# A rotary step whose halves ScalarE swaps, and one group of queries kept in natural order

## The chip, the cores and the metric

The kernel runs on one core of a Trainium2 chip. A core has TensorE (PE in the profile, with its weight loads shown apart as PEld), VectorE (DVE), ScalarE (ACT), GpSimd (POOL), and SyncE (SP), which here issues all DMAs. The metric is the device time of one execution in microseconds (us).

## The reference

A decoder trunk of two layers over 1024 tokens of width 1024. The first layer is gated linear attention. The second makes keys and values once, projects queries for three groups of eight heads, and lets each group attend through a dilated window; then the groups are mixed by their log sum of exponentials, gated, projected out, and normalized. What the change touches is the rotary step of the keys and queries and the score product:

```python
def rope(x, pos):
    half = e // 2
    ang = pos[:, None] * inv[None, :]          # one angle for each of 64 pairs
    x1, x2 = x[..., :half], x[..., half:]
    return concatenate([x1 * cos - x2 * sin, x2 * cos + x1 * sin])

SWA_GROUPS = ((128, 1), (512, 4), (2048, 16))  # window, dilation of groups 0, 1, 2
# group with dilation d: the sequence is split into d interleaved subsequences
# (t = i*d + r); each is a plain band of 128 keys, swept in blocks of 128 queries
scores = einsum('brnqgpe,brnkge->brngpqk', qb, kcat)
```

The head width is 128, so a head's queries lie with one component on each of the 128 partitions and the tokens along the free dimension. The two halves that the rotary step mixes are partitions 0 to 63 and 64 to 127.

## The kernel before

All large products are made in three matmuls: each fp32 operand is split into a high and a low part (`wh` and `wl` for weights, `x1h` and `x1l` for the residual stream), and high by high, high by low, low by high add up in PSUM (`mm3`, L642). These run in a fast fp32 mode, 512 tokens at a time. The attention products (`lv` scores, `ms` transposes, `po` sums over values) are plain fp32 matmuls; the profile shows each of those as two matmul records with a weight load for each.

Layer B works unit by unit, a unit being one query head in all three groups (`u` from 0 to 7). `q_proj(u)` projects three 128x1024 pages of queries, `Q[0]` to `Q[2]`, each in two halves of 512 tokens. A half is 24 matmuls into one of two PSUM banks (`acc`), and `rope` (L1194) takes it out: DVE multiplies it by the cosines into `t1`, then in two 64-partition instructions multiplies the swapped halves by the sines into `t2`, and DVE or POOL adds the two into the page. The page is stored in the order of its group (`to_group`, L1165): group 0 in token order, group 1 with the four subsequences one after the other (256 tokens each), group 2 in 16 short runs. Keys `K` go through the same `rope`, in 12 halves. `scores(u)` (L1327) multiplies a block of queries, as the stationary operand, with its keys, as the moving one; DVE adds the mask and takes the row extreme, ACT takes the exponential. `attend(u)` scales the probabilities by the mixing weights `cw`, which make a round trip through DRAM, transposes them, and multiplies with the values.

The order of work is made at build time. Every call is recorded with the engines that may run it (`S.vp` is DVE or POOL, `S.va` is DVE or ACT), and `Sched.order` (L254) simulates the engines with a table of costs (`cost`, L543), taking at each step the instruction that can start first, with a priority from program order. So one edit moves many instructions. All instructions are issued at L452, which is why the profile names tiles and not lines. The unit loop is L1515 to L1528: while PE scores unit `u`, its gaps are filled with projections of the next unit.

Of the kernel before, what the change touches and what calls it, by code (L numbers as in the profile page):

```python
# [597 lines left out]
def trunk(tc, xT, wP, wA, wA12, wAv3, w2, wO, wK, wV0, wV12, wB, wOB, par_d,  # L598
          ident_d, lmask_d, cos_d, sin_d, bmask_d, rmask_d, tri_d, lnr_d, out):
    S = Sched(tc, lat=LAT, pad=PAD)  # L600
# [6 lines left out]
    t2 = S.pool("t2")  # L607
    t1 = S.pool("t1", side="right")
# [9 lines left out]
    def page(pool, dt, name):  # L618
        return pool.tile([128, T], dt, name=name, tag="pg", bufs=16)

    def hs(half):
        return slice(half * 512, half * 512 + 512)


    def load_w(src):
        with S.later(-WEIGHTS):
            return load_w_now(src)
# [21 lines left out]
    def proj_cols(w, xs, r, acc):  # L649
        hi, lo = w  # L650
        for kt in range(NK):
            xh, xl = xs[kt]
            mm3(acc, hi[:, kt, :], lo[:, kt, :], xh[:, r], xl[:, r], kt)

    def project(piece, xs, evac, halves=(0, 1)):
        w = load_w(piece)
        for half in halves:
            acc = ps.tile([128, 512], F32, name="acc", bufs=2)
            proj_cols(w, xs, hs(half), acc)
            with S.later(-EVAC):  # L660
                evac(half, acc)
# [391 lines left out]
    def small(name, tag, bufs, dt=F32, shape=(128, 512)):  # L1053
        return hp.tile(list(shape), dt, name=name, tag=tag, bufs=bufs)
# [110 lines left out]
    def to_group(pg, g, half):  # L1165
        if g == 2:
            return pg.rearrange("p (e a n) -> p n a e", e=16, a=8)[:, half * 4:half * 4 + 4]
        n = 512 // DIL[g]
        return pg.rearrange("p (r i) -> p i r", r=DIL[g])[:, half * n:half * n + n, :]

    def tok_view(ap, g):
        if g == 2:
            return ap.rearrange("p (n a e) -> p n a e", n=4, a=8)
        return ap.rearrange("p (i r) -> p i r", r=DIL[g])

    def layer_b(xs, early):
# [14 lines left out]
        sinT = page(p0, F32, "sinT")  # L1191
        S.sync.dma_start(sinT, sin_d)

        def rope(pg, g, half, acc):  # L1194
            r = hs(half)
            t1 = small("t1", "t1", 2)
            S.vector.tensor_mul(t1, acc, cosT[:, r])
            t2 = small("t2", "t2", 2)
            S.vector.tensor_mul(t2[0:64, :], acc[64:128, :], sinT[64:128, r])
            S.vector.tensor_mul(t2[64:128, :], acc[0:64, :], sinT[0:64, r])  # L1200
            S.vp.tensor_add(to_group(pg, g, half), tok_view(t1, g), tok_view(t2, g))

        K = [[page(p0, F32, f"K{c}{g}") for g in range(3)] for c in range(2)]
        V = [[None] * 3 for _ in range(2)]
# [98 lines left out]
        def q_proj(u):  # L1303
            Q = [page(p0, F32, "Q") for _ in range(3)]
            U[u]["Q"] = Q
            for g in range(3):
                project(wB[u, g], xs, lambda half, acc: rope(Q[g], g, half, acc))


        def g_proj(u):  # L1310
# [9 lines left out]

        def pieces(P, g, j0):
            p, o = P[g, j0 + 1]
            n = 1 if g or not j0 else 2
# [2 lines left out]

        def scores(u):  # L1327
            Q, Kc = U[u]["Q"], K[u // 4]
            P = {}
            sts = hp.tile([128, 2, 24], F32, name="sts", bufs=2)  # L1330
            for g in (2, 1, 0):
                step = 8 if g == 2 else 2
                for j0 in range(0, 8, step):
                    sc = ps.tile([128, 512], F32, name="lv", bufs=2)
                    p = small("P", "a", 13)
                    o = 0
                    if g == 2:
                        with S.group():
                            for j in range(8):
                                for s in range(2):  # L1340
                                    x = s * 512 + j * 64
                                    o = place(j)
                                    S.tensor.matmul(sc[s * 64:s * 64 + 64, o:o + 64], Q[g][:, x:x + 64],
                                                     Kc[g][:, x:x + 64], start=True, stop=True)
                    for j in range(j0, j0 + step):
                        qc, kc, nk = BL[g][j]
                        col = column(g, j)
                        if g == 2:
                            o = place(j)
                        P[g, j] = p, o  # L1350
                        px = p[:, o:o + nk]
                        if g < 2:
                            S.tensor.matmul(sc[:, o:o + nk], Q[g][:, qc:qc + 128], Kc[g][:, kc:kc + nk],
                                             start=True, stop=True)
                        mk = rmask if g == 2 else bmask[:, 256 - nk:]

                        S.vector.tensor_tensor_reduce(
                            out=px, in0=sc[:, o:o + nk], in1=mk, scale=-QSCALE, scalar=-LOWEST,
                            op0=OP.add, op1=OP.min, accum_out=sts[:, 0, col:col + 1])
                        S.scalar.activation(px, px, AF.Exp, scale=-1.0, bias=sts[:, 0, col:col + 1],  # L1360
                                             accum_out=sts[:, 1, col:col + 1])
                        o += nk
                    if g < 2:

                        prev, own = pieces(P, g, j0)
                        S.vector.copy_predicated(own, above.to_broadcast(list(own.shape)), prev)
            U[u]["P"] = P

# [232 lines left out]
def _arrays(inputs):  # L1601
    import numpy as np

    f4 = np.float32
    c = np.ascontiguousarray
    w_in = np.asarray(inputs["gla_w_in"])[0]

    def cols(w, first, n=128):

        return w[:, first:first + n].reshape(8, 128, n).transpose(1, 0, 2)  # L1610

    r = np.arange
    w_out = np.asarray(inputs["gla_w_out"])[0]
    w_kv = np.asarray(inputs["w_kv"])
    swi = np.asarray(inputs["swa_w_in"])[0]
    swo = np.asarray(inputs["swa_w_out"])[0]
    w2 = np.asarray(inputs["gla_w_a2"])[0]
    a = {
        "xT": c(np.asarray(inputs["x"])[0].T),
        "wP": c(np.concatenate([cols(w_in, 1024, 256), cols(w_in, 3072, 16)], axis=2)),  # L1620
        "wA": c(np.stack([np.stack([cols(w_in, f) for f in (h * 128, 512 + h * 128, 2048 + h * 256,
                                                             2176 + h * 256)]) for h in range(4)])),
        "wA12": c(cols(w_in, 1280, 512)),
        "wAv3": c(cols(w_in, 1792, 256)),
        "w2": c(np.concatenate([w2] * 6, axis=0)),
        "wO": c(np.stack([cols(w_out, e * 128) for e in range(8)])),
        "wK": c(np.stack([cols(w_kv, e * 128) for e in range(6)])),
        "wV0": c(cols(w_kv, 768, 256)),
        "wV12": c(cols(w_kv, 1024, 512)),
        "wB": c(np.stack([np.stack([cols(swi, f * 1024 + h * 128) for f in range(4)]) for h in range(8)])),  # L1630
        "wOB": c(np.stack([cols(swo, e * 128) for e in range(8)])),
        "par": c(np.concatenate([np.asarray(inputs[n]).reshape(-1, 128).T
                                 for n in ("ln_g", "ln_b", "gla_norm_g", "gla_b_a2")], axis=1)),

        "lnr": c(np.stack([np.broadcast_to(np.asarray(inputs[n])[1], (128, 1024)) for n in ("ln_g", "ln_b")])),
    }

    a["ident"] = np.eye(128, dtype=f4)
    j, i = np.meshgrid(r(128) % 32, r(32), indexing="ij")
    lm = np.zeros((128, NLEV - 2, 32), f4)  # L1640
    for n, L in enumerate(LEVELS[2:]):
        lm[:, n, :] = (j // (2 * L) == i // (2 * L)) & (j % (2 * L) < L) & (i % (2 * L) >= L)
    lm[:, NLEV - 3, :] = j == i
    a["lmask"] = lm
    inv = f4(10000.0) ** (-(r(64, dtype=f4) * f4(2.0)) / f4(128.0))
    ang = r(1024).astype(f4)[None, :] * inv.astype(f4)[:, None]
    cs, sn = np.cos(ang).astype(f4), np.sin(ang).astype(f4)
    a["cos"] = c(np.concatenate([cs, cs]))
    a["sin"] = c(np.concatenate([sn, -sn]))
    q, k = np.meshgrid(r(128), r(256), indexing="ij")  # L1650
    rel = 128 + q - k
    a["bmask"] = np.where((rel >= 0) & (rel <= 128), f4(0), f4(NEG)).astype(f4)
    q, k = np.meshgrid(r(128) % 64, r(64), indexing="ij")
    tq, tk = (128 * (i % 8) + 16 * (i // 8) for i in (q, k))
    i, j = np.arange(128)[:, None], np.arange(128)[None, :]
    a["tri"] = np.stack([j > i, j < i, j >= i], axis=1).astype(f4)
    a["rmask"] = np.where(tk <= tq, f4(0), f4(NEG)).astype(f4)
    return a
# [27 lines left out]
```

## Time and profile before

| what | value |
|---|---|
| time, median of 3 runs | 1154.25 us (1153.87 to 1154.63) |
| span of the profiled execution | 1152.7 us |
| PE busy | 1142.8 us, 99% of the span |
| DVE busy | 820.3 us, 71% |
| ACT busy | 449.1 us, 39% |
| POOL busy | 188.0 us, 16% |

The span runs from the first to the last instruction of one profiled execution; the median lies 1.5 us above it, and that execution has no other time of its own. The busy time of PE counts a matmul until its modelled end, and matmuls overlap, so the pace of PE is read from the distance between starts and not from durations. On the other engines busy time is what the instruction held the engine.

### The profile page before, as it was taken

What the parts mean: (1) busy time and instruction counts of PE and PEld (TensorE: products, weight loads), DVE (VectorE), ACT (ScalarE), POOL (GpSimd) and SP (SyncE); (2) the same over time, 40 slices, a digit from 0 to 9 for tenths busy, and PEclk for the clock granted to TensorE, in tenths of its full rate; (3) what the DMA queues carried; (4) which work ended last, traced back from release to release, by engine and by line L of the source; (5) the groups of instructions that cost most, each with busy time, mean ns of one, the idle gap of its engine ahead of it and who ended that gap; (6) DMA issues with size and microseconds to landing.
All of it is one profiled execution on the core that took longest, in us unless ns stands there. A gap on an engine that the chain in (4) does not pass through costs nothing.

```text
span 1152.7 us, 19731 instructions
## 1 busy us (share of the span) xinstructions
PE 1142.8 (99%) x7780; PEld 975.2 (85%) x7780; DVE 820.3 (71%) x1634; ACT 449.1 (39%) x929; POOL 188.0 (16%) x139
## 2 busy tenths in 40 slices
PE   9999999999999999999999999999999999999997
PEld 9888888889988888888988888888888888888876
DVE  6286862786966699764366868686777878767678
ACT  5355431646463335311214242424222443444342
POOL 1000100112011120211020303030211312212200
PEclk9999999999999999999999999999999999999999
DMA  7211222111144365443611111121141111134544
GB/s 256 71 38 38 74 79 87 38 61 51 57 171 140 137 214 158 166 143 103 208 47 34 51 38 57 38 50 45 38 165 39 38 21 38 39 96 126 193 136 182
DMA packets 93372, 108.39 MB, mean 94 GB/s; under 512 B 43648, under 2 KB 61952, under 8 KB 93280
## 3 DMA queue, kind: packets, MB, share of 16 engines
q1 hardware_dynamic: 93280, 107.13, 29.6%
q8 instruction: 61, 1.00, 0.4%
q14 instruction: 31, 0.25, 0.1%
HBM read 85.94 MB, written 21.17 MB: 93 GB/s over the span
## 4 chain that ended last, share of the span: by engine, by line
PE 93%; DVE 4%; DMA 2%; ACT 1%; issue 1%; POOL 0%; DVEq 0%; ACTq 0%
PE acc L452 63%; PE po L452 9%; PE lv L452 8%; PE vac L452 7%; PE ms L452 4%; PE pro L452 2%; DMA wf<-in_wOB 2%; DVE rt L452 1%; DVE wl L452 1%; DVE x1l L452 0%; ACT wh L452 0%; DVE P L452 0%; DVE lnA L452 0%; ACT woh L452 0%; DVE wol L452 0%
## 5 line engine op out<-in xcount | busy, mean ns | idle before, releaser
L452 PE MATMUL acc<-x1h,wh 128*128 128x512 f32 x608 | 252.3, 415 | 0.0
L452 PE MATMUL acc<-x1h,wl 128*128 128x512 f32 x608 | 237.6, 391 | 0.0
L452 PE MATMUL acc<-x1l,wh 128*128 128x512 f32 x608 | 237.1, 390 | 0.0
L452 ACT ACTIVATE wh<-wf 128x1024 fp32r<-128x1024 f32 (+2 forms) x104 | 108.1, 1040 | 281.0 <-PE acc L452 194.8
L452 POOL TENSOR_TENSOR wl<-wf,wh 128x1024 fp32r<-128x1024 f32 x39 | 93.5, 2397 | 553.1 <-ACT wh L452 414.8
L452 ACT ACTIVATE P<-P,sts 128x128 f32<-128x128 f32 (+2 forms) x192 | 81.5, 426 | 139.6 <-DVE sts L452 139.3
L452 PEld LDWEIGHTS acc<-x1h,wl 128*128 128x128 f32 x608 | 114.1, 188 | 24.5
L452 PEld LDWEIGHTS acc<-x1l,wh 128*128 128x128 f32 x608 | 114.5, 188 | 21.3
L452 PEld LDWEIGHTS acc<-x1h,wh 128*128 128x128 f32 x608 | 114.4, 188 | 21.1
L452 DVE TENSOR_TENSOR wl<-wf,wh 128x1024 fp32r<-128x1024 f32 (+2 forms) x66 | 83.4, 1265 | 58.2 <-ACT wh L452 48.0
L452 PE MATMUL acc<-xh,wh 128*128 128x512 f32 x256 | 101.8, 397 | 0.0
L452 PE MATMUL acc<-xh,wl 128*128 128x512 f32 x256 | 99.8, 390 | 0.0
L452 PE MATMUL acc<-xl,wh 128*128 128x512 f32 x256 | 99.7, 390 | 0.0
L452 DVE TENSOR_TENSOR t<-acc,cosT 128x512 f32<-128x512 f32 x60 | 41.4, 689 | 65.7 <-PE acc L452 65.7
L452 DVE TENSOR_TENSOR t<-acc,sinT 64x512 f32<-64x512 f32 x120 | 82.5, 688 | 1.6
L452 PE MATMUL lv<-K,Q 128*64 128x64 f32 (+2 forms) x512 | 70.2, 286 | 0.0
L452 DVE CUSTOM_DVE_ANT_0 P<-lv,bmask 128x256 f32<-128x256 f32 (+1 forms) x128 | 46.7, 379 | 25.1 <-PE lv L452 23.7
L452 PEld LDWEIGHTS lv<-K,Q 128*128 128x128 f32 (+1 forms) x512 | 53.8, 163 | 10.0 <-issue 1.6
L452 PE MATMUL acc<-ogh,wh 128*128 128x512 f32 x152 | 60.1, 395 | 0.0
L452 PE MATMUL acc<-ogh,wl 128*128 128x512 f32 x152 | 59.2, 389 | 0.0
L452 PE MATMUL acc<-ogl,wh 128*128 128x512 f32 x152 | 59.2, 389 | 0.0
L452 PEld LDWEIGHTS acc<-xh,wl 128*128 128x128 f32 x256 | 48.0, 188 | 10.2
(252 smaller groups left out, 2233.4 us busy)
## 6 DMA issues: line engine op xcount, KB each, us to landing
wf<-in_wB SPq DMA_DIRECT2D x32, 512.0 KB
wf<-in_wA SPq DMA_DIRECT2D x24, 512.0 KB
wf<-in_wO SPq DMA_DIRECT2D x16, 512.0 KB
wf<-in_wOB SPq DMA_DIRECT2D x16, 512.0 KB
wf<-in_wV SPq DMA_DIRECT2D x12, 512.0 KB
res<-in_xT SPq DMA_DIRECT2D x16, 256.0 KB
x1d<-rt SPq DMA_DIRECT2D x16, 256.0 KB
out<-rt SPq DMA_DIRECT2D x16, 256.0 KB
```

The source lines that it names most:

```text
L452: getattr(handle[o.eng], meth)(*[conv(a) for a in args], **{k: conv(v) for k, v in kw.items()})
```

## The change

`rope` makes the swap a job of its own. ACT copies partitions 64 to 127 of the PSUM bank into partitions 0 to 63 of `t2`, and 0 to 63 into 64 to 127; one multiplication over all 128 partitions, on DVE or POOL, then applies the sines, and the addition stays. The sine table changes the sign of its halves to fit. Keys are stored as before. Of the queries, group 1 is now stored in token order, by a plain addition, and `scores` reads each block of its stationary operand with a step of four elements (16 bytes).

```diff
-        def rope(pg, g, half, acc):
+        def rope(pg, g, half, acc, walked=(0, 1, 2)):
             r = hs(half)
             t1 = small("t1", "t1", 2)
             S.vector.tensor_mul(t1, acc, cosT[:, r])
             t2 = small("t2", "t2", 2)
-            S.vector.tensor_mul(t2[0:64, :], acc[64:128, :], sinT[64:128, r])
-            S.vector.tensor_mul(t2[64:128, :], acc[0:64, :], sinT[0:64, r])
-            S.vp.tensor_add(to_group(pg, g, half), tok_view(t1, g), tok_view(t2, g))
+            S.scalar.copy(t2[0:64, :], acc[64:128, :])
+            S.scalar.copy(t2[64:128, :], acc[0:64, :])
+            S.vp.tensor_mul(t2, t2, sinT[:, r])
+            if g in walked:
+                S.vp.tensor_add(to_group(pg, g, half), tok_view(t1, g), tok_view(t2, g))
+            else:
+                S.vp.tensor_add(pg[:, r], t1, t2)
...
-                project(wB[u, g], xs, lambda half, acc: rope(Q[g], g, half, acc))
+                project(wB[u, g], xs, lambda half, acc: rope(Q[g], g, half, acc, (0, 2)))
...
             Q, Kc = U[u]["Q"], K[u // 4]
+            Q = [Q[0], Q[1].rearrange("p (i r) -> p r i", r=4), Q[2]]
...
                         if g < 2:
-                            S.tensor.matmul(sc[:, o:o + nk], Q[g][:, qc:qc + 128], Kc[g][:, kc:kc + nk],
+                            qb = Q[1][:, qc // 256, qc % 256:qc % 256 + 128] if g else blk(Q[0], j)
+                            S.tensor.matmul(sc[:, o:o + nk], qb, Kc[g][:, kc:kc + nk],
                                              start=True, stop=True)
...
-    a["sin"] = c(np.concatenate([sn, -sn]))
+    a["sin"] = c(np.concatenate([-sn, sn]))
```

Layer A keeps its order; in layer B the planner places work anew. Three places of the new order follow.

On DVE, the rotary step of the first half of group 1's queries in unit 1 (`Q_6090` before, `Q_6130` now). Before:

```order
L452 TENSOR_TENSOR t1_6076<-acc_6029,cosT_4371 128x512
L452 TENSOR_TENSOR t2_6081<-acc_6029,sinT_4375 64x512 x2
L452 TENSOR_TENSOR Q_6090<-t1_6076,t2_6081 128x128x4
L452 TENSOR_TENSOR mnB_6095<-nat_5964 128x8
L452 TENSOR_TENSOR mnB_6095<-mnB_6095,sts_5841 128x8
```

Now:

```order
L452 TENSOR_TENSOR t1_6117<-acc_6052,cosT_4371 128x512
L452 TENSOR_TENSOR t2_6119<-t2_6119,sinT_4375 128x512
L452 TENSOR_TENSOR Q_6130<-t1_6117,t2_6119 128x512
L452 TENSOR_TENSOR t1_6156<-acc_6113,cosT_4371 128x512
L452 TENSOR_TENSOR wl_6163<-wf_5976,wh_6154 128x1024
L452 TENSOR_TENSOR t2_6161<-t2_6161,sinT_4375 128x512
```

The two 64-partition products of the PSUM bank have become one product of `t2` with itself as input and output, the addition writes in one run of 512, and a split of weights (`wl`) that POOL made elsewhere stands on DVE.

On ACT, from the last exponential of unit 0 to the mixing weights' scalings (`P<-P,cw`). Before:

```order
L452 ACTIVATE P_6011,sts_5841<-P_6011,sts_5841 128x256 x2
L452 ACTIVATE wh_6033<-wf_5810 128x1024
L452 ACTIVATE ew_6101<-ew_6101 128x24
L452 ACTIVATE wh_6129<-wf_5927 128x1024
L452 ACTIVATE P_5947<-P_5947,cw_6116 128x128
L452 ACTIVATE P_5957<-P_5957,cw_6116 128x256
```

Now, from the copies of the fourth half to those of the fifth:

```order
L452 ACTIVATE t2_6161<-acc_6113 64x512 x2
L452 ACTIVATE P_5949<-P_5949,cw_6104 128x128
L452 ACTIVATE P_5949<-P_5949,cw_6104 128x256
L452 ACTIVATE P_5880<-P_5880,cw_6104 128x128
L452 ACTIVATE P_5880<-P_5880,cw_6104 128x256
L452 ACTIVATE P_5893<-P_5893,cw_6104 128x128
L452 ACTIVATE P_5911<-P_5911,cw_6104 128x128
L452 ACTIVATE P_5928<-P_5928,cw_6104 128x256
L452 ACTIVATE P_5968<-P_5968,cw_6104 128x256
L452 ACTIVATE P_6003<-P_6003,cw_6104 128x256
L452 ACTIVATE t2_6213<-acc_6150 64x512 x2
```

Each half now has a pair of copies in ACT's queue, and the pair of the fifth half (`acc_6150`) stands behind all of ACT's scalings of unit 0.

On PE, scores of group 1 in unit 1 (`K01` are its keys) between the projections. Before:

```order
L452 MATMUL acc_6398<-x1h2_4296,wl_6042 128x512
L452 MATMUL lv_6415<-K01_5008,Q_6090 128x128
L452 MATMUL lv_6396<-K01_5008,Q_6090 128x256
L452 MATMUL acc_6398<-x1h3_4320,wh_6033 128x512
L452 MATMUL acc_6398<-x1l3_4335,wh_6033 128x512
L452 MATMUL acc_6398<-x1h3_4320,wl_6042 128x512
L452 MATMUL lv_6415<-K01_5008,Q_6090 128x256
L452 MATMUL lv_6429<-K01_5008,Q_6090 128x128
```

Now:

```order
L452 MATMUL acc_6417<-x1h1_4254,wl_6066 128x512
L452 MATMUL lv_6370<-K01_5010,Q_6130 128x256
L452 MATMUL lv_6413<-K01_5010,Q_6130 128x256
L452 MATMUL acc_6417<-x1h2_4296,wh_6056 128x512
L452 MATMUL acc_6417<-x1l2_4310,wh_6056 128x512
L452 MATMUL acc_6417<-x1h2_4296,wl_6066 128x512
L452 MATMUL lv_6442<-K01_5010,Q_6130 128x128
```

The same matmuls stand in a slightly other interleaving; each `Q_6130` is the operand read with a step.

## The prediction

> **What bounds the kernel now.** I read the page's first parts, then what PE waits for, then the pace at which PE's matmuls start, then the groups by form.
>
> ```profile
> span 1152.7 us, 19731 instructions
> PE 1142.8 (99%) x7780; PEld 975.2 (85%) x7780; DVE 820.3 (71%) x1634; ACT 449.1 (39%) x929; POOL 188.0 (16%) x139
> ...
> PE 93%; DVE 4%; DMA 2%; ACT 1%; issue 1%; POOL 0%; DVEq 0%; ACTq 0%
> ```
>
> PE is busy for all but 10 us, and 93% of the chain that ended last is PE. Busy time alone proves little, since a matmul's end is modelled. The waits of PE, complete:
>
> ```profile
> PE pro L452 <- DVE Dg L452: 1.2, 1, 1.2
> PE po L452 <- DVE PT L452: 0.8, 1, 0.8
> PE ms L452 <- DVE sum L452: 0.5, 2, 0.2
> PE ms L452 <- ACT sum L452: 0.2, 1, 0.2
> ```
>
> That is 2.7 us in the whole program. The first is the start, the last two the normalizations; only the 0.8 us, in the last unit's `attend`, lies in work that this change moves. A short wait could still hide inside modelled ends, so I checked the pace of starts in layer B:
>
> ```profile
> 710.99 0.39 PE L452 MATMUL acc<-x1l,wh 128*128 128x512 f32 x1
> 711.22 0.39 PE L452 MATMUL acc<-x1h,wl 128*128 128x512 f32 x1
> ...
> 731.15 0.81 PE L452 MATMUL lv<-K,Q 128*128 128x128 f32 x4
> 731.62 0.58 PE L452 MATMUL acc<-x1h,wh 128*128 128x512 f32 x1
> 732.03 0.39 PE L452 MATMUL acc<-x1l,wh 128*128 128x512 f32 x1
> ```
>
> A 512-token matmul starts 0.227 us after the one before, all through. At 731.15 PE leaves the projections for four fp32 score records (two of 128 columns, two of 256) and goes back. From 731.15 to 732.03 are 0.88 us; at 0.112 us for 128 fp32 columns (from rows further down) and twice that for 256 the content is 0.224 + 0.448 + 0.227 = 0.90 us. So going back and forth between the two kinds costs nothing that shows. PE is full, and what DVE does is hidden behind it.
>
> **The change, part by part.** The durations:
>
> ```profile
> L452 DVE TENSOR_TENSOR t<-acc,sinT 64x512 f32<-64x512 f32 x120 | 82.5, 688 | 1.6
> L452 DVE TENSOR_TENSOR t<-acc,cosT 128x512 f32<-128x512 f32 x60 | 41.4, 689 | 65.7 <-PE acc L452 65.7
> L452 DVE TENSOR_TENSOR rt<-rt,R 128x512 f32<-128x512 f32 x24 | 16.0, 683 | 0.3 <-ACT R L452 0.3
> L452 POOL TENSOR_TENSOR Q<-t,t 128x512 f32<-128x512 f32 x8 | 11.3, 1411 | 0.0
> L452 ACT ACTIVATE th<-acc 128x512 f32<-128x512 f32 x16 | 9.4, 588 | 20.6 <-PE acc L452 20.6
> L452 DVE TENSOR_TENSOR wl<-wf,wh 128x1024 fp32r<-128x1024 f32 (+2 forms) x66 | 83.4, 1265 | 58.2 <-ACT wh L452 48.0
> ...
> 686.60 0.69 DVE L452 TENSOR_TENSOR Q<-t,t 128x512 f32<-128x512 f32 x1
> ...
> 698.60 1.09 DVE L452 TENSOR_TENSOR Q<-t,t 128x512 f32<-128x512 f32 x1
> ```
>
> *The products with the sines.* DVE loses 120 instructions of 688 ns, 82.5 us. In their place are 60 products of two SBUF operands over 128 partitions, nearest to the `rt<-rt,R` row: in the new order 51 on DVE at 683 ns (34.8 us) and 9 on POOL at 1.41 us (12.7 us).
>
> *Group 1's additions.* The row at 686.60 is group 0 written in one run, the one at 698.60 is group 1 written with a step of 256 elements: 0.40 us more. Sixteen additions lose it, 6.4 us of DVE and POOL. The planner hands some of the time back: DVE takes 14 weight splits (`wl`, 1.27 us each, 17.7 us) from POOL. DVE ends near 820 - 83 + 35 - 6 + 18, about 785 us, or less busy by 35 us. What it is worth: nothing, because PE waited 0.8 us in all for DVE in this stretch.
>
> *The copies.* 120 of them, 64x512 from PSUM on ACT. No row has this form. `th<-acc`, 512 elements a partition from PSUM, takes 588 ns, and DVE's rows show 64 partitions costing as much as 128 (688 and 689), so I take 588; half of it is a lower bound, and the 688 that DVE needs for the same swapped read an upper one. That is 71 us on ACT, 449 to about 520 of 1152. Cover: a bank is taken again 24 matmuls later, 24 x 0.227 = 5.4 us, while the cosine product and the pair of copies run side by side and free it in 1.2 us, against 0.69 + 2 x 0.69 = 2.1 before. The addition follows after 1.18 + 0.68, no later than before. Worth nothing; if ACT comes late, see the third case.
>
> *The order of PE.* The matmuls are the same. They change between projections and fp32 work oftener (176 stretches of projections against 161 in PE's order); at no cost that shows, or 0.01 us of rounding each, this is at most 0.15 us.
>
> *The strided operand.* 64 score matmuls of group 1 (four subsequences, two blocks, eight units), 128 weight loads, now read their 128 columns with a step of 16 bytes. No load in the trace does. The rows to bound it by:
>
> ```profile
> L452 PEld LDWEIGHTS lv<-K,Q 128*128 128x128 f32 x256 | 45.7, 189 | 7.7
> L452 PEld LDWEIGHTS lv<-K,Q 128*64 128x64 f32 x256 | 8.1, 138 | 2.3 <-issue 1.6 <-DVE zz L452 0.7
> ...
> 720.35 2.40 PE L452 MATMUL po<-PT,V 128*128 128x128 f32 x20
> ...
> 725.31 3.29 PE L452 MATMUL po<-PT,V 128*128 128x128 f32 x28
> ```
>
> A load of 64 columns takes 138 ns and one of 128 takes 189, so a column costs 0.8 ns and a dense load occupies about 102 ns behind the running matmul. The two `po` rows bound it from below: the 20 records at 720.35 are group 1 and write PSUM with just this step of four fp32 elements, the 28 at 725.31 are group 0 and write densely. Spacing: (2.40 - 0.275) / 19 = 0.112 us against (3.29 - 0.275) / 27 = 0.112. On the same engine, the same step at the same pace of under one element per 0.8 ns costs nothing: lower end 0. From above: DVE's stepped addition pays 0.40 / 512 = 0.79 ns more per element; on 128 columns 101 ns, a load of 203. A load hides behind the matmul record in front of it. By the new order, 40 of the 128 loads stand behind a record of 128 fp32 columns (0.112 us), 5 behind a shorter one, all others behind 0.21 us or more: 40 x (203 - 112) + 5 x 101 = 4.1 us. With no cover at all it is 128 x 101 = 12.9 us. I take 0, because the `po` row shares engine, step and pace with the new read, while DVE's row is a write with a 64 times longer step.
>
> **The sum.** 1152.7 span + 0 (DVE) + 0 (ACT) + 0.15 (order) + 0 (loads) = 1152.9; the last unit's wait of 0.8 us may go or double. The shown median lies 1.5 us above the span: 1154.4 us, no change. Own range 1153.4 to 1156.
>
> **The rivals.** *Slower by the strided loads:* the place is the second record of each 128-column score, where the load has only 0.112 us of cover. For: the stepped DVE row, SBUF like this read. Against: the `po` rows. It decides from 2.3 / 45 = 51 ns of exposed time a load, a load of some 165 ns. Price 4.1 us: 1158.5; up to 1167 without cover. The Trainium skill, page "SBUF — State Buffer", section "Specifications (TRN2)", speaks for this case: SBUF has 16-byte lines and full bandwidth needs at least two hits per line, whereas a step of four fp32 gives one. The page "PSUM — Partial Sum Buffer", same section, has a like rule for 8-byte lines, that any non-contiguous pattern slows matmuls significantly; the two `po` spacings of 0.112 us disagree with that one, so I do not let the rule decide.
>
> *Slower by ACT's queue:* the fifth half's copies stand behind nine scalings that wait for the mixing weights from DRAM.
>
> ```profile
> ACT P L452 <- DMA cw<-cwd: 5.0, 2, 4.5
> ...
> 702.13 3.98 ACT L452 ACTIVATE P<-P,cw 128x128 f32<-128x128 f32 x11 [0.48 <-DMA cw<-cwd]
> ```
>
> Eleven scalings take 3.98 us, nine 3.3. If `cw` lands as the half ends, its bank is free 3.3 + 1.2 = 4.5 us later, and PE needs it after another half and eight transposes (16 records), 5.4 + 1.8 = 7.2 us. So 2.7 us are spare. A wait of 4.5 us, the longest here, would stop PE for 1.8 us; two of them in the seven units make 3.6 us: 1158.0. Against: the second wait was 0.5 us.
>
> *Faster:* a less busy DVE removes the 0.8 us wait and rounding in the scores. Beyond that PE has nothing to lose but its 64 stepped matmuls and the 1.9 us at start and normalizations, which the change does not reach. Price 1153.6, within the bound; over 2.3 us it would take a tail that shortens, and there the rows are layer norm's.
>
> *The change doesn't do what it says:* the planner could have kept as many DVE instructions; the order rules it out.
>
> **How the numbers follow.** No change 0.51 (1154.4); strided loads 0.38 (1158.5); ACT's queue 0.05 (1158.0); faster 0.06. The likeliest gives the time. The range reaches to the load case with part of its bounds, 1152.6 to 1161; outside are 6 in 100 below and some 8 above. Faster and slower begin at 0.2%, 2.3 us, about what a measurement of this kernel can tell from no change: faster 0.06, same 0.51, slower 0.38 + 0.05 = 0.43.
>
> **What would show it.** Loads right: `lv<-K,Q` loads of 128 columns stay at 189 ns and PE's spacing inside group 1's scores at 0.112 us; wrong: longer loads, and a second 128-column record that starts 0.2 us after the first. Copies: `t<-acc` on ACT near 588 ns, 120 times. DVE: near 785 us, `Q<-t,t` of group 1 at 0.69. PE's waits stay below 4 us; a new row "PE acc <- ACT t" there would be the third case. The forecast falls if PE's starts thin out anywhere in layer B.

## The result, and the profile after

The changed kernel takes 1164.6 us (median of 4 runs, 1163.9 to 1164.7), the kernel before 1154.1 us in runs beside it (1153.6 to 1154.6). The ratio is 1.0092, with a 95% interval from 1.0078 to 1.0107: slower by about 10.5 us, outside the range of the forecast. The changed kernel's page and TensorE's waits, complete:

```profile
span 1162.9 us, 19850 instructions
PE 1150.4 (99%) x7780; PEld 984.7 (85%) x7780; DVE 781.8 (67%) x1608; ACT 515.8 (44%) x1035; POOL 155.0 (13%) x119
...
PE 92%; DVE 4%; DMA 2%; ACT 1%; issue 1%; SPq 0%; DVEq 0%; ACTq 0%
```

```profile
PE ms L452 <- DVE P L452: 2.6, 3, 0.9
PE pro L452 <- DVE Dg L452: 1.2, 1, 1.2
PE ms L452 <- DVE sum L452: 0.5, 2, 0.2
PE acc L452 <- DVE wol L452: 0.3, 1, 0.3
PE ms L452 <- ACT sum L452: 0.2, 1, 0.2
```

DVE is relieved as planned and ACT takes the copies, but the span is 10.2 us longer and PE is still busy for 99% of it. The waits sum to 4.8 us against 2.7. A row is new: three times the transposes (`ms`) wait for DVE's scaled probabilities (`P`), 2.6 us together, while the 0.8 us for `PT` are gone. So most of the 10 us cannot be a wait that this list shows. The groups by form (busy us, mean ns, idle before and what ended it) show where else to look:

```profile
L452 PEld LDWEIGHTS lv<-K,Q 128*128 128x128 f32 x256 | 57.1, 253 | 7.2 <-DVE sts L452 0.9
L452 PE MATMUL lv<-K,Q 128*128 128x128 f32 x80 | 20.9, 342 | 0.0
L452 ACT ACTIVATE t<-acc 64x512 f32<-64x512 f32 x120 | 71.2, 593 | 92.3 <-DVE t L452 64.8 <-PE acc L452 17.9 <-DVE mnB L452 8.3
L452 DVE TENSOR_TENSOR t<-t,sinT 128x512 f32<-128x512 f32 x51 | 47.7, 935 | 33.2 <-ACT t L452 33.1
```

The score loads take 253 ns on the mean, 189 before. Half of the 256 still read densely, so a stepped one is near 2 x 253 - 189 = 317 ns. The timeline shows what that does to the pace of TensorE, at the first block of a subsequence of group 1 (128 columns, two records):

```profile
663.26 0.63 PE L452 MATMUL lv<-K,Q 128*128 128x128 f32 x2
663.73 0.94 PE L452 MATMUL po<-PT,V 128*128 128x128 f32 x7
```

The two records and their loads fill 663.73 - 663.26 = 0.47 us, or 0.235 us a record; the forecast had 0.112. A busy PE hides this, since a matmul that waits for its weights counts as busy. The lines on ACT hold the second clue, taken up below: the copies were mostly held by DVE's `t`, the cosine product of the same bank.

### The profile page after: what moved, and what is told of

It reads as the page before. It is cut to its first block, busy times and chain, and to the rows that moved or that the text cites. A ratio compares the mean times of both kernels' runs of the same rounds, so it can differ in the third digit from the quotient of the medians.

```text
span 1162.9 us, 19850 instructions
## 1 busy us (share of the span) xinstructions
PE 1150.4 (99%) x7780; PEld 984.7 (85%) x7780; DVE 781.8 (67%) x1608; ACT 515.8 (44%) x1035; POOL 155.0 (13%) x119
## 4 chain that ended last, share of the span: by engine, by line
PE 92%; DVE 4%; DMA 2%; ACT 1%; issue 1%; SPq 0%; DVEq 0%; ACTq 0%
PE acc L452 60%; PE lv L452 10%; PE po L452 9%; PE vac L452 7%; PE ms L452 4%; PE pro L452 2%; DVE rt L452 1%; DMA wf<-in_wOB 1%; DVE wl L452 1%; DMA nat<-std 1%; DVE x1l L452 0%; ACT wh L452 0%; DVE lnA L452 0%; DVE t L452 0%; ACT woh L452 0%
## 5 line engine op out<-in xcount | busy, mean ns | idle before, releaser
L452 DVE TENSOR_TENSOR wl<-wf,wh 128x1024 fp32r<-128x1024 f32 (+2 forms) x80 | 99.7, 1247 | 61.1 <-ACT wh L452 51.1
L452 POOL TENSOR_TENSOR wl<-wf,wh 128x1024 fp32r<-128x1024 f32 x25 | 59.8, 2390 | 556.3 <-PE ms L452 305.0
L452 ACT ACTIVATE t<-acc 64x512 f32<-64x512 f32 x120 | 71.2, 593 | 92.3 <-DVE t L452 64.8
L452 PE MATMUL lv<-K,Q 128*64 128x64 f32 (+2 forms) x512 | 77.7, 299 | 0.0
L452 PEld LDWEIGHTS lv<-K,Q 128*128 128x128 f32 (+1 forms) x512 | 65.2, 195 | 9.2 <-DVE P L452 1.1
L452 DVE TENSOR_TENSOR t<-t,sinT 128x512 f32<-128x512 f32 x51 | 47.7, 935 | 33.2 <-ACT t L452 33.1
```

What stands on the lines that cost most here:

```text
L452: getattr(handle[o.eng], meth)(*[conv(a) for a in args], **{k: conv(v) for k, v in kw.items()})
```

## The experiments

Two theories stood at the start. **Loads:** the 128 stepped weight loads cost TensorE 6 to 7 us, and what is left comes from the new order of the other engines. **Order:** the loads are hidden, and the new order on DVE and ACT thins out TensorE. The diffs below are against the changed kernel; experiments that build on another say so.

### The rotary step alone

```diff
-                project(wB[u, g], xs, lambda half, acc: rope(Q[g], g, half, acc, (0, 2)))
+                project(wB[u, g], xs, lambda half, acc: rope(Q[g], g, half, acc))
...
-            Q = [Q[0], Q[1].rearrange("p (i r) -> p r i", r=4), Q[2]]
...
-                            qb = Q[1][:, qc // 256, qc % 256:qc % 256 + 128] if g else blk(Q[0], j)
+                            qb = Q[g][:, qc:qc + 128]
```

> The rotary step alone: the copies on ScalarE and the one product with the sines as in the change, but group 1's queries go back to group order and the scores read them densely. If the strided loads cost the most (theory: 128 loads at about 310 to 330 ns instead of 190, some 6 to 7 us of TensorE), the time falls to 1156 to 1158 us, since 2 to 4 us of the new order stay, and all 256 loads of 128 columns stand at 189 ns. If it is the new order of VectorE and ScalarE that thins out TensorE (rival), the time stays near 1163.

Measured: 1158.55 us, ratio 1.0037 (1.0023 to 1.0051) to the kernel before, loads at 189 ns. Neither theory had it: just above the first one's 1158, far under the second one's 1163. Without one stepped load the rotary step costs 4.6 us. TensorE's waits in it begin with

```profile
PE ms L452 <- DVE P L452: 4.0, 3, 1.4
```

### The stepped read alone

```diff
             t2 = small("t2", "t2", 2)
-            S.scalar.copy(t2[0:64, :], acc[64:128, :])
-            S.scalar.copy(t2[64:128, :], acc[0:64, :])
-            S.vp.tensor_mul(t2, t2, sinT[:, r])
+            S.vector.tensor_mul(t2[0:64, :], acc[64:128, :], sinT[64:128, r])
+            S.vector.tensor_mul(t2[64:128, :], acc[0:64, :], sinT[0:64, r])
```

(with the sine table of before)

> The other part alone: the rotary step of before (VectorE's 120 half products with the sines), but group 1's queries in natural order, read with a step of 16 bytes. Loads theory: 1160 to 1161 us, the 128 stepped loads at 310 to 330 ns, ScalarE near 449 us. Rival (order): 1154, the same as before, though the loads are longer.

Measured: 1163.69 us, 1.0084 (1.0069 to 1.0099), loads at 254 ns, ACT busy 447 us. The loads cost time whatever the rotary step is; 9.7 us is more than either theory's figure. This kernel's order differs from both others, so the sum of the two parts (4.6 + 9.7) need not be, and isn't, the whole. It has three waits of TensorE that the kernel before lacks, 0.9 us together (for `sts` 0.5, for `sg` and `P` 0.2 each). And its loads are covered less well: 53 of the 128 stepped ones stand behind a record of 128 columns, against 40 in the changed kernel, and 5 behind a shorter one. With 0.235 us for a stepped load an estimate is 53 x 0.123 + 5 x 0.133 us, and up to 0.025 us for each of the other 70: 7.2 to 8.9 us, with the waits 8.1 to 9.8. The 9.7 us lie at its upper end.

### The changed kernel with dense weights

Only the address pattern of the 64 weights differs from the changed kernel; every engine has the same instructions in the same places. Group 1's scores then belong to other tokens' queries.

```diff
-            Q = [Q[0], Q[1].rearrange("p (i r) -> p r i", r=4), Q[2]]
...
-                            qb = Q[1][:, qc // 256, qc % 256:qc % 256 + 128] if g else blk(Q[0], j)
+                            n, r = qc % 256 // 128, qc // 256
+                            qb = Q[1][:, n * 512 + r * 128:n * 512 + r * 128 + 128] if g else blk(Q[0], j)
```

> The changed kernel with every instruction at its place on every engine, but the 64 stepped weights of group 1's scores are taken as 128 neighbouring columns of the same half of the page: group 1's scores then use other tokens' queries than they should, which changes no duration but the load's. Loads theory: 1157 to 1158 us, so 6 to 7 below the change, loads of 128 columns all at 189 ns. Rival (order): 1164, as the change.

Measured: 1157.19 us, 1.0030 (1.0019 to 1.0042). So in an unchanged order the step costs 1164.6 - 1157.2 = 7.4 us, and everything else in the change 3.2 us. Its span, and the same place in its timeline:

```profile
span 1155.4 us, 19850 instructions
```

```profile
662.49 0.39 PE L452 MATMUL lv<-K,Q 128*128 128x128 f32 x2
662.71 1.50 PE L452 MATMUL po<-PT,V 128*128 128x128 f32 x12
```

Two records in 0.22 us again. Its waits still hold `PE ms <- DVE P` with 2.6 us, as the changed kernel's do: the waits do not come from the loads.

### What a step costs: 8, 12 and 32 bytes

The kernel with dense weights, with other steps in place of its pattern, one line for each of three runs:

```diff
+  qb = Q[1].rearrange("p (i r) -> p r i", r=2)[:, r % 2, n * 256 + r // 2 * 128:n * 256 + r // 2 * 128 + 128] if g else blk(Q[0], j)  # 8 bytes
+  qb = Q[1][:, n * 512 + r:n * 512 + r + 382:3] if g else blk(Q[0], j)               # 12 bytes
+  qb = Q[1].rearrange("p (i r) -> p r i", r=8)[:, 2 * r + n] if g else blk(Q[0], j)  # 32 bytes
```

> The changed kernel, order untouched, with a step of 8 bytes instead of 16 in the 64 weights of group 1's scores (they take other tokens' queries). If a load is slowed by reading one element of each 16-byte line (the Trainium skill, page SBUF - State Buffer, section Specifications (TRN2), asks for at least two hits a line for full bandwidth), two hits a line give loads near 189 ns and 1157 to 1158 us. If any step slows it alike, loads stand at 310 to 330 ns and the time at 1164; something between, if the cost goes with the bytes passed over, would be about 250 ns and 1160.

> The changed kernel, order untouched, with a step of 12 bytes in the weights of group 1's scores (other tokens' queries): one or two elements of each 16-byte line. If a load's time goes with the lines that it touches beyond two elements a line, 128 columns touch 96 lines against 64 with a step of 8 bytes and 128 with 16: occupied about three quarters of the 230 ns at 16 bytes, 170 to 180 ns, so PEld records near 260 and a time between 1158 and 1165, near 1161. If the price is all or nothing by the step (any above 8 bytes), 310 to 330 ns and 1164 to 1165.

> The changed kernel, order untouched, with a step of 32 bytes in the weights of group 1's scores (other tokens' queries). Two theories fit what 8, 12 and 16 bytes gave (records started 118, 174 and 230 ns apart where a load held them up): 1.8 ns for each 16-byte line touched, or 14.5 ns for each byte of the step. By lines, 128 columns touch 128 lines at 16 bytes and at 32: loads stay at 309 to 330 ns and the time at 1164 to 1165. By bytes, a load occupies some 460 ns, is recorded at 540 to 560, and hides behind nothing: about 1180 or more.

Measured: 1157.94 us (8 bytes), 1160.72 (12 bytes), 1164.43 (32 bytes). For each the group of the 256 loads (half of them dense), and from the timeline the same first block of a subsequence. At 8 bytes:

```profile
L452 PEld LDWEIGHTS lv<-K,Q 128*128 128x128 f32 x256 | 47.9, 192 | 9.2 <-DVE sts L452 0.9
```

```profile
662.49 0.40 PE L452 MATMUL lv<-K,Q 128*128 128x128 f32 x2
662.73 1.50 PE L452 MATMUL po<-PT,V 128*128 128x128 f32 x12
```

At 12 bytes:

```profile
L452 PEld LDWEIGHTS lv<-K,Q 128*128 128x128 f32 x256 | 53.1, 221 | 7.2 <-DVE sts L452 0.9
```

```profile
662.89 0.51 PE L452 MATMUL lv<-K,Q 128*128 128x128 f32 x2
663.24 1.50 PE L452 MATMUL po<-PT,V 128*128 128x128 f32 x12
```

At 32 bytes:

```profile
L452 PEld LDWEIGHTS lv<-K,Q 128*128 128x128 f32 x256 | 57.8, 257 | 7.2 <-DVE sts L452 0.9
```

```profile
662.71 0.64 PE L452 MATMUL lv<-K,Q 128*128 128x128 f32 x2
663.18 1.28 PE L452 MATMUL po<-PT,V 128*128 128x128 f32 x10
```

Together, with the stepped load worked out as twice the mean less 189, and the distance of one record from these rows:

| step | 16-byte lines under 128 columns | stepped load, ns | distance of a record, us | time, us |
|---|---|---|---|---|
| 4 bytes (dense) | 32 | 189 | 0.11 | 1157.2 |
| 8 bytes | 64 | 195 | 0.12 | 1157.9 |
| 12 bytes | 96 | 253 | 0.175 | 1160.7 |
| 16 bytes (the change) | 128 | 317 | 0.235 | 1164.6 |
| 32 bytes | 128 | 325 | 0.235 | 1164.4 |

The theory of lines foresaw all three; the rival of bytes wanted 460 ns of occupancy and 1180 us at 32 bytes, and falls. Where a load sets the pace it takes about 1.8 ns for each 16-byte line that it touches (0.175 us for 96 lines, 0.235 for 128). With two elements a line, 0.12 us against 0.11 dense, it is already so near the pace of a dense load that this row fits the price but does not test it.

### The step on the moving operand

The kernel with dense weights, its keys of group 1 read with the step instead:

```diff
-                            S.tensor.matmul(sc[:, o:o + nk], qb, Kc[g][:, kc:kc + nk],
+                            kb = Kc[1].rearrange("p (i r) -> p r i", r=4)[:, kc // 256, :nk] if g else Kc[0][:, kc:kc + nk]
+                            S.tensor.matmul(sc[:, o:o + nk], qb, kb,
```

> The changed kernel, order untouched, with 128 neighbouring columns as the weights of group 1's scores, and the step of 16 bytes moved to the other operand: the keys of group 1 are read with a step of four elements (so group 1's scores belong to other tokens). If a step costs the read of SBUF itself, the moving operand pays as the weights did: 128 moving columns need some 230 ns in place of 112, and group 1's 64 matmuls (24,576 columns in the eight units, each read twice by an fp32 matmul) cost far more than the loads did, about 24 us or more beside the 1157 of the dense run. If only weight loads are slowed, because a matmul in fp32 takes its columns slower than a load does, the time stays at 1157 to 1158.

Measured: 1180.05 us, 1.0221 (1.0201 to 1.0242). The 64 matmuls stream 12,288 columns, each twice, which makes 24,576 reads (the expectation gives that number as columns, but it counts both passes already). They cost 1180.05 - 1157.19 = 22.9 us, 0.93 ns a read. The rows of two groups of records show it without the sum (here and in the dense run):

```profile
L452 PE MATMUL lv<-K,Q 128*128 128x128 f32 x80 | 23.4, 380 | 0.0
```

```profile
L452 PE MATMUL lv<-K,Q 128*128 128x128 f32 x80 | 15.9, 280 | 0.0
```

So it is the read of SBUF that is slow, whichever operand makes it. A moving operand pays more in all: it is read oftener here (24,576 columns against 128 loads of 128, 16,384), and nothing hides it.

### The order: what the planner did not know

The other 3.2 us (4.6 in the rotary step alone) come with the waits for `P`. The changed kernel's timeline of DVE, then of ACT and of PE, around the first of them:

```profile
882.44 0.69 DVE L452 TENSOR_TENSOR t<-acc,cosT 128x512 f32<-128x512 f32 x1 [1.93 <-PE acc L452]
883.05 0.16 DVE L452 TENSOR_TENSOR mnB<-nat 128x8 f32<-128x8 f32 x1
883.24 0.17 DVE L452 TENSOR_TENSOR mnB<-mnB,sts 128x8 f32<-128x8 f32 x1
884.46 0.69 DVE L452 TENSOR_TENSOR t<-t,sinT 128x512 f32<-128x512 f32 x1 [1.04 <-ACT t L452]
885.18 1.10 DVE L452 TENSOR_TENSOR Q<-t,t 128x512 f32<-128x512 f32 x1
886.12 0.18 DVE L452 TENSOR_TENSOR ew<-mnB,nat 128x16 f32<-128x16 f32 x1
...
887.91 0.69 DVE L452 TENSOR_TENSOR P<-P,cw 128x512 f32<-128x512 f32 x1
```

```profile
883.23 1.20 ACT L452 ACTIVATE t<-acc 64x512 f32<-64x512 f32 x2 [4.16 <-DVE mnB L452]
```

```profile
887.46 0.39 PE L452 MATMUL acc<-x1h,wl 128*128 128x512 f32 x1
888.66 0.66 PE L452 MATMUL ms<-ident,P 128*128 128x128 f32 x4 [0.82 <-DVE P L452]
```

ACT's copies do not run beside the cosine product: it ends at 882.44 + 0.69 = 883.13, they start at 883.23. (The row names `mnB`, which overlaps the product's end, as what ended ACT's wait; in 30 other cases the profile names the product.) In none of the 60 halves of this trace do the two overlap: in 54 both copies come after (0.135 us on the median), in 6 the cosine product stands between the two copies. The Trainium skill, page "PSUM — Partial Sum Buffer", section "PSUM bank collisions raise a hardware error", states a rule that would make this so: the compiler back end's scheduler adds a dependency between any two instructions on different engines that touch the same bank in the same 32 partitions, reads and writes alike. The 60 pairs agree.

DVE then stands 1.04 us at the sine product, waiting for the copies, and behind it in its queue are the addition and the whole chain from `mnB` to the mixing weights, which could have gone on when `mnB` was done at 883.4. It goes on at 886.12, the scaling of `P` ends at 888.6, and the transposes, placed by the planner for an earlier time, stop PE for 0.82 us. The planner takes reads of one bank as independent, and reckons 0.49 us for a copy that takes 0.593. Four runs told it the truth, on the changed kernel or on the rotary step alone:

```diff
# start: a copy also counts as a reader of t1, the cosine product's output (both copies)
             S.scalar.copy(t2[0:64, :], acc[64:128, :])
+            S.ops[-1].reads.append(t1)
# cost of ACT
-        c = 0.105 + n * 0.83e-3 + 0.093 * pointers - 0.04 * psum
+        c = 0.105 + n * 0.83e-3 + 0.093 * pointers - 0.04 * psum + 0.1 * (psum and meth == "copy")
```

Both truths, the rotary step alone:

> The rotary step alone, dense reads, and the planner told what the traces showed of the copies: 0.59 us each where it reckons 0.49, and a start after the cosine product of the same bank (it had them side by side). If TensorE's waits for the scalings by cw in the last three units (4.0 us) come from an order planned on wrong times, they go, and the time falls from 1158.5 to 1154 or 1155.5. If the rotary step itself is what makes the chain late (each half's queries ready about 0.8 us later), whatever the order, it stays at 1157.5 to 1159.

Measured: 1153.72 us, 0.9996 (0.9986 to 1.0005): the 4.6 us are gone. TensorE's waits sum to 1.9 us here and to 6.5 in the rotary step alone, which is the whole difference. Both truths in the whole change:

> The whole change with the same two truths told to the planner. If the two causes add up, it loses the waits of TensorE for the scalings (2.6 us) and keeps the loads: 1161 to 1162.5. If the planner's belief doesn't matter, 1164 to 1165.

Measured: 1159.86 us, 1.0046 (1.0031 to 1.0061), 1.1 us better than the lower figure expected. The causes add up: between these two kernels lies the stepped read, 6.1 us, and between this and the changed kernel the order, 4.7 us. Of the 4.7, TensorE's waits show 3.2 (4.8 against 1.6); the rest is not placed. In no run was the planner told what a stepped load costs. Each truth by itself, on the rotary step alone:

> The rotary step alone with dense reads (as in the first run), and the planner told only that a copy takes 0.59 us; it still believes that the copies and the cosine product of a bank run side by side. If the late start of the copies (94 ns after the cosine product's end in most halves, where the planner has both at once) is what it misses, the waits for the scalings stay and the time is 1157 to 1159. If 0.1 us a copy was enough, 1153.5 to 1155.

> The same with the other truth alone: the planner starts a copy after the bank's cosine product, and reckons 0.49 us a copy. If the start is the cause, 1153.5 to 1155 and no wait of TensorE for P in the last units; if not, 1157 to 1159.

Measured: with the cost 1156.34 us, 1.0022 (1.0012 to 1.0031); with the start 1153.46 us, 0.9999 (0.9989 to 1.0008). The start does it all; the cost brings about half, for which neither theory had a place. No run moved the order by a change that tells the planner nothing true, so what another order brings by chance is not measured. For the start speaks that the waits for `P` are gone in all three runs that told it. TensorE's waits with the start told, complete, and its transposes at the first of the three places:

```profile
PE pro L452 <- DVE Dg L452: 1.2, 1, 1.2
PE ms L452 <- DVE sum L452: 0.2, 1, 0.2
PE ms L452 <- ACT sum L452: 0.2, 1, 0.2
```

```profile
884.54 0.39 PE L452 MATMUL acc<-x1h,wl 128*128 128x512 f32 x1
884.77 0.60 PE L452 MATMUL ms<-ident,P 128*128 128x128 f32 x4
```

The transposes start 0.23 us after the matmul before them, the ordinary pace. DVE still stands 0.76 us at the sine product there, but the next step from `mnB` to the mixing weights (`ew`) now goes ahead of it.

## Why the prediction was wrong

*What bounds the kernel* held: PE is full, and busy DVE time is worth nothing. With the start told, the rotary step alone runs with 37 us less DVE work (820.3 to 782.9) and takes the same time.

*The products with the sines, the additions, the weight splits:* the sum held, in part by luck. DVE was forecast near 785 us and has 781.8. But a sine product takes DVE 935 ns on the mean, not 683: 38 of the 51 took 0.69 us, and the 13 that ran beside a POOL instruction 1.65 us, in all 12.9 us more than reckoned. The additions made up for it: on DVE they fell from 72.5 us to 50.2, where 6 us were forecast, with 24 of 52 beside POOL before and 4 of 58 now. That POOL is the cause is read from the trace; no run separated it.

*The strided operand* is the step that failed, by its choice and by its bounds. I took 0 from the `po` rows, which write PSUM with the same step on the same engine; the loads read SBUF, and that turned out to be what matters. The upper end, a load of 203 ns worked out from DVE's stepped addition, was no upper end either: the load occupies 0.235 us. With that in the prediction's own sum, 40 loads behind 0.112 us cost 40 x 0.123 = 4.9 us, 5 behind a shorter one 5 x (0.235 - 0.102) = 0.7, and the 83 behind 0.21 us or more up to 0.025 us each, 2.1: 5.6 to 7.7 us. The runs gave 6.1 and 7.4. So the rival of the loads had the place, the mechanism and the cover right, and its price of 4.1 us was too small. The rule of two hits a line, from the page "SBUF — State Buffer" of the Trainium skill, section "Specifications (TRN2)", which the prediction cited and set aside, is borne out: 195 ns for a load with two elements a line, 317 with one. Setting it aside because the PSUM rule beside it disagreed with a row was the fault, since the two speak of different memories.

*The copies:* the duration held (593 ns for the 588 taken, ACT at 515.8 us for some 520), "run side by side" did not. A bank is free after 0.69 + 0.1 + 1.2 = 2.0 us, not 1.2, and this cost nothing at the bank, as the cover of 5.4 us said: no row "PE acc <- ACT t" appears. But "the addition follows no later than before" fell with it. Before, a half with as long an addition went

```profile
877.77 0.69 DVE L452 TENSOR_TENSOR t<-acc,cosT 128x512 f32<-128x512 f32 x1 [1.07 <-PE acc L452]
878.48 1.39 DVE L452 TENSOR_TENSOR t<-acc,sinT 64x512 f32<-64x512 f32 x2
879.90 1.11 DVE L452 TENSOR_TENSOR Q<-t,t 128x512 f32<-128x512 f32 x1
```

that is 2.13 us from the cosine product to the addition; now it is 885.18 - 882.44 = 2.74 us, with DVE standing still in between. Over the 60 halves the median is 2.13 us before, 2.82 now, and 2.82 too with the start told, where no time is lost. So a later addition costs nothing by itself; an order planned for an earlier one does. I named ACT's queue behind the scalings as the danger, and it was DVE's queue behind the copies. This second missing term is worth 3.2 us in the changed kernel (1157.2 with dense weights against 1154.0 before).

*The sum:* 1152.9 us of span was forecast, 1162.9 came. The step adds 7.5 (1162.9 - 1155.4); the rest is 2.7 (1155.4 - 1152.7), of which the waits for `P` are 2.6, less the 0.8 for `PT` that went; about 0.9 us of small terms are not placed. *The range* ended at 1161.0, though the load case itself reached to 1167 without cover. The loads alone, at the 7.4 us measured, make 1161.5, already outside; the loads and the order at once had no case.

## What to carry to other kernels

Bound an access that the trace lacks by rows of the same memory and the same kind of access, and count what covers it; one that is near on the engine but lies in another memory bounds nothing. Before costing two engines on one PSUM bank as parallel, look for a wait between them, and for what stands in the queue behind the one that waits. Where an order is planned from a table, an edit that adds a new kind of work needs its durations and its waits in the table, or the order is made for a machine that doesn't exist: here that was worth 4.6 us in the rotary step alone and 4.7 in the whole change, nearly half the loss.

## What the runs showed of the hardware

TensorE's reads of SBUF, in these fp32 matmuls, go by 16-byte lines: 1.8 ns a line where a weight load sets the pace (96 and 128 lines in 0.175 and 0.235 us), no further price for a step of 32 bytes (0.235), and 0.93 ns more for each column read of a moving operand with a step of 16 bytes. Its writes to PSUM with a step of 16 bytes cost nothing (0.112 us for 128 columns, with the step and without). Reads of one PSUM bank by ACT and by DVE never overlapped, in 60 halves of 60; the program waits between them. DVE's sine products, with both operands in SBUF, took 0.69 us, and 1.65 on the mean beside a POOL instruction; three cosine products beside POOL, with one operand in PSUM, took 0.68.
